# A hybrid decoder trunk on one core: every tile moved to another place in its memory row

## The chip, the cores and the metric

The kernel runs on one core of a Trainium2 chip. The metric is the time of one execution on the device, in microseconds (us). A core has five engines with instruction streams of their own: TensorE (PE in the profile; its weight loads have a row of their own, PEld), VectorE (DVE), ScalarE (ACT), GpSimd (POOL) and SyncE (SP). The on-chip memory has 128 partitions; a tile takes the same bytes in each of its partitions, so its place is one byte address, the same in all rows. PSUM is the memory that matmuls write.

A matmul has two operands in that on-chip memory: the *stationary* one, a block of up to 128x128 values that is loaded into the array by a weight load (LDWEIGHTS), and the *moving* one, up to 512 columns that stream past it (MATMUL). The profile names a matmul `out<-moving,stationary`: `acc<-whi,gh` streams a piece of the tile `whi` past a block of `gh`.

## The reference, cut to what matters

Two layers over 256 tokens of width 1024, in float32:

```
x = x + 0.5 * swiglu_ffn(x, ffn1)          # 1024 -> 2 x 2816 -> 1024
h = rms_norm(x);  z = h @ w_in             # one wide input projection
y = sum_i sigmoid(gate_i(h)) * (branch_i @ P_i)   # stick-breaking, latent, sparse attention
x = x + y @ w_out
x = x + 0.5 * swiglu_ffn(x, ffn2)
```

Nothing in the change touches what is computed.

## The kernel before, in words

**Products.** Each float32 product is made of three matmuls of a reduced type: every operand is held as a high part and a low remainder, and `mm3` (lines 528 to 532) issues high x high (L530), high x low (L531) and low x high (L532). In the large projections the activations are stationary and the weights move. So the stationary order within one `mm3` is: high block, high block again, low block; every one of the three has its own weight load.

**Stationary tiles.** The activations lie transposed, 128 values by 128 rows to a block, and each block is 512 bytes of a memory row: `hThi`, `hTlo` (`new_T`, L540; two buffers each) for the normed input of a block; `gh0`, `gl0`, `gh1`, `gl1` (L675) for the gated activation of an FFN; `oh`, `ol` (`new_oT`, L766) for the output of an attention branch; `cT` (L873) for the latent.

**Moving tiles.** Weights come as slabs of 128x1024 values. A slab arrives in `raw` tiles of 512 columns (L503, issued on SP's queue), ACT writes the high part into `whi` (L514, L817) and DVE the remainder into `wlo` (L515, L819); there are four buffers of each. In the mixer the probabilities `wr` move past `V`, and the scores' masks and constants lie in `rt`. A transpose is a matmul too: the data is stationary and `ident` moves.

**Order.** Each layer is FFN, mixer (attention), FFN. PE's instructions stand in the order in which the program writes them. In the mixer a planner works out one order for PE, ACT and DVE from its own cost estimates, and that order is fixed (a manual schedule); in the FFNs ACT's and DVE's order is left to the framework. None of the planner's costs looks at an address.

**Places.** Tiles are taken from pools, and pools lie behind one another in the memory row: `cp` (constants), `sm` (small statistics, five buffers of each of four kinds, 64 bytes each), `wp` (whi, wlo, raw), `hp` (rows of x, `hThi`, `hTlo`, `rn`), and then `fp` in an FFN or `mp` in a mixer, in the same space. Within a pool each kind of tile lies behind the last one. In `cp` there is one tile of 32 bytes, `g_col` (L408), the first layer's gain as a column, which ACT writes once (L413) and DVE reads for the first transposes (L555). All other sizes in front of `wp` add up so that with these 32 bytes every tile of `wp`, `hp`, `fp` and `mp` named above begins 32 bytes behind a multiple of 512.

The places, as the remainder of a tile's first byte by 512:

| tile | before | after |
|---|---|---|
| whi, wlo, raw, x, h, mq, nq, nk | 32 | 0 |
| ident | 320 | 320 |
| rt | 352 | 320 |
| hThi | 32 | 64 |
| hTlo | 32 | 128 |
| gh0, gl0 | 32, 32 | 192, 256 |
| gh1, gl1 | 32, 32 | 320, 384 |
| V, cT, zw | 32 | 128 |
| oh, ol | 32, 32 | 256, 320 |
| wf, wr, th, qk, pc, Vc | 32 | 320 |

The column "after" is the sum of the sizes that the diff leaves: 32 bytes less in front of everything, then the free spaces.

One group of matmuls has always had its stationary operand at another remainder than its moving one: the compressed scores of the sparse branch (L1668), whose stationary blocks are cut out of `zkh` and `zkl` at columns 32, 0, 128 and 96, while `nq` moves.

Of the kernel before, what the change touches and what calls it, by code (L numbers as in the profile page):

```python
# [10 lines left out]
F = mybir.dt.float32  # L11
R = mybir.dt.float32r
# [5 lines left out]
S = 256  # L18
DEPTH = 2
DFF = 2816  # L20
EPS = 1e-6
NT = 2
KT = D // 128
# [333 lines left out]
def decoder_trunk(ctx, tc, x_in, wts, gains, lcon, cst, out, depth=DEPTH):  # L357
# [4 lines left out]
    cp = ctx.enter_context(tc.tile_pool(name="cp", bufs=1))  # L362
    sm = ctx.enter_context(tc.tile_pool(name="sm", bufs=5))
    wp = ctx.enter_context(tc.tile_pool(name="wp", bufs=W_BUFS))
    hp = ctx.enter_context(tc.tile_pool(name="hp", bufs=2))
# [4 lines left out]
    def acc_tile():  # L370
        return pb.tile([128, 512], F, tag="ps", name="acc")

    def tp_tile():
        return pb.tile([128, 512], F, tag="ps", name="tp")

    def att_tile():
        return pb.tile([128, 512], F, tag="ps", name="att")

    def big_tile(name, dt=F, shape=(128, D)):
        return hp.tile(list(shape), dt, tag="hy", name=name, bufs=6)  # L380

# [18 lines left out]
    def load_x(t, cols=(0, 1)):  # L400
        for c in cols:
            cs = slice(c * 512, (c + 1) * 512)
            nc.sync.dma_start(xs[t][:, cs], x_in[t * 128:(t + 1) * 128, cs])


    g_row = big_tile("grow")[0:8, 0:128]
    nc.sync.dma_start(g_row, gains[0].rearrange("(k p) -> k p", k=8))
    g_col = cp.tile([128, 8], F, name="g_col")  # L408

    def first_gain():  # L410
        tp = tp_tile()
        nc.tensor.transpose(tp[:, 0:8], g_row, ident[0:8, 0:8])
        nc.scalar.activation(g_col, tp[:, 0:8], AF.Copy)  # L413
# [93 lines left out]
    def load_slab():  # L507
        base, n, name = slab_at(pos[0])
        pos[0] += 1
        hi, lo = slab_tiles()  # L510
        for c in range(0, n, RAW):
            m = min(RAW, n - c)
            raw = load_raw(base, c, m)
            nc.scalar.activation(hi[:, c:c + m], raw[:, :m], AF.Copy)  # L514
            nc.vector.tensor_tensor(lo[:, c:c + m], raw[:, :m], hi[:, c:c + m], op=OP.subtract)  # L515
        return name, (hi, lo)

    def next_slab():
        while pos[0] < len(stream) and len(ready) < 1 + AHEAD:
            ready.append(load_slab())  # L520
        return ready.pop(0)[1]


    def split(hi, lo, src):
        nc.scalar.activation(hi, src, AF.Copy)  # L525
        nc.vector.tensor_sub(lo, src, hi)  # L526

    def mm3(o, a, b, start=False, stop=False):

        nc.tensor.matmul(o, a[0], b[0], start=start, stop=False)  # L530
        nc.tensor.matmul(o, a[0], b[1], start=False, stop=False)  # L531
        nc.tensor.matmul(o, a[1], b[0], start=False, stop=stop)  # L532
# [5 lines left out]
        return r  # L538

    def new_T():  # L540
        return (hp.tile([128, KT, 128], R, tag="hThi", name="hThi"),
                hp.tile([128, KT, 128], R, tag="hTlo", name="hTlo"))

    def to_T(dst, src, halves=(0, 1), tmp=None):

        for half in halves:
            tp = tp_tile()
            for j in range(4):
                k = half * 4 + j
                nc.tensor.transpose(tp[:, j * 128:(j + 1) * 128], src[:, k * 128:(k + 1) * 128], ident)  # L550
            k = slice(half * 4, half * 4 + 4)
            v = tp.rearrange("p (a b) -> p a b", a=4)
            if tmp is not None:
                u = tmp[:, half * 512:half * 512 + 512].rearrange("p (a b) -> p a b", a=4)
                nc.vector.tensor_tensor(u, v, g_col[:, k, None].to_broadcast([128, 4, 128]), op=OP.mult)  # L555
                v = u
            split(dst[0][:, k, :], dst[1][:, k, :], v)
# [19 lines left out]
    def enter():  # L577

        return [big_tile("h") for _ in range(NT)], [new_T() for _ in range(NT)], [None] * NT
# [71 lines left out]
    def ffn(l, gi):  # L651
        if l == 0 and gi == 0:
            nxt[0] = hs, hT, rn = enter()
            gain_n[0] = 1
            first_gain()
            ready.append(load_slab())
            load_x(0, (1,))
            to_T(hT[0], xs[0], tmp=hs[0])
            sl = [next_slab()]
            load_x(1)  # L660
            for t in range(NT):
                rn[t] = norm_scale(t)
            h1 = dict(tmp=hs[1])
            hs = [None, xs[1]]
            steps = [(0, 0, 0), (0, 0, 1), (0, 1, 0), (1, 0, 0), (1, 0, 1), (1, 1, 0), (0, 1, 1), (1, 1, 1)]
            h1_at = (2, 0), (2, 2)
        else:
            sl = []
            steps = [(t, part, q) for t in range(NT) for part in range(2) for q in range(2)]
            h1_at = (2, 0), (2, 3)  # L670
            hs, hT, rn = nxt[0]
            h1 = {}
        with ExitStack() as es:
            fp = es.enter_context(tc.tile_pool(name="fp", bufs=2))
            gT = [(fp.tile([128, DFF // 128, 128], R, name=f"gh{t}", bufs=1),  # L675
                   fp.tile([128, DFF // 128, 128], R, name=f"gl{t}", bufs=1)) for t in range(NT)]
            todo = []

            def glu(t, a, b, f0, fn):
                s = fp.tile([128, 512], F, tag="sil", name="sil")  # L680
                nc.scalar.activation(s[:, :fn], a[:, :fn], AF.Silu, scale=rn[t][:, 0:1])
                g = fp.tile([128, 512], F, tag="g", name="g", bufs=3)
                nc.vector.scalar_tensor_tensor(g[:, :fn], b[:, :fn], rn[t][:, 0:1], s[:, :fn], op0=OP.mult, op1=OP.mult)  # L683
                todo.append((t, g, f0, fn))

            def flush():
                if todo:
                    t, g, f0, fn = todo.pop(0)
                    tp = tp_tile()
                    q = fn // 128  # L690
                    for j in range(q):
                        nc.tensor.transpose(tp[:, j * 128:(j + 1) * 128], g[:, j * 128:(j + 1) * 128], ident)  # L692
                    k0 = f0 // 128
                    split(gT[t][0][:, k0:k0 + q, :], gT[t][1][:, k0:k0 + q, :],
                          tp[:, :fn].rearrange("p (a b) -> p a b", a=q))

            f0, fn = FFN_CHUNKS[0]
            g = KT // 2
            assert g * fn == 1024
            sl += [next_slab() for _ in range(4 - len(sl))]  # L700
            ab = {}
            for i, (t, part, q) in enumerate(steps):
                if q == 0:
                    ab[t, part] = acc_tile()
                a = ab[t, part]
                for k in range(q * g, q * g + g):
                    if (i, k) in h1_at:
                        to_T(hT[1], hs[1], (h1_at.index((i, k)),), **h1)
                    mm3(a[:, :fn], cut(hT[t], A, k, A),
                        cut(sl[part * 2 + q], A, slice((k % g) * fn, (k % g + 1) * fn)),  # L710
                        start=k == 0, stop=k == KT - 1)
                if part == 1 and q == 1:
                    glu(t, ab[t, 0], a, f0, fn)

            def hook(i):
                if i in (3, 5):
                    flush()

            for ci, (f0, fn) in enumerate(FFN_CHUNKS[1:]):
                if ci == 1:  # L720
                    with tc.issue_after(last_dma[0]):
                        if l == 0 and gi == 0:
                            load_consts()
                        load_gain()
                        if gi == 0:
                            load_lc(l)
                if ci == 3 and gi == 0:
                    make_tables()
                a = {}
                drain(chunk(fn, KT, hT, a.__setitem__), hook)  # L730
                drain(chunk(fn, KT, hT, lambda t, b: glu(t, a[t], b, f0, fn)))

            def between(k):
                if k in (2, 3):
                    flush()
            out_rows(gT, DFF // 128, between, last=l == depth - 1 and gi == 2)


    def mixer(l):
        es = ExitStack()  # L740
        mp = es.enter_context(tc.tile_pool(name="mp", bufs=1))
# [21 lines left out]
        def bc(a, H):  # L763
            return a[:, None, :].to_broadcast([a.shape[0], H, a.shape[-1]])

        def new_oT():  # L766
            return (mp.tile([128, 4, S], R, tag="oh", name="oh", bufs=2),
                    mp.tile([128, 4, S], R, tag="ol", name="ol", bufs=2))

        last_act = []  # L770

# [100 lines left out]

        cT = mp.tile([128, 2, NT, 3, 128], R, tag="r3", name="cT")  # L873
        cT = cT[:, 0], cT[:, 1]
        o_sb, o_mla, o_nsa = new_oT(), new_oT(), new_oT()
        small = mp.tile([128, 256], F, name="small")
        krg = [small[:, 56 * t:56 * t + 56] for t in range(NT)]
        ev_hT, ev_rn, ev_cT, ev_krg = events(2), [Tok(2.0), Tok(4.0)], events(NT), events(NT)
# [950 lines left out]
```

## Time and profile before

| what | value |
|---|---|
| three runs | 1319.73, 1321.48, 1323.20 us; median 1321.48 us |
| the profiled execution | 1320.05 us, of which the span of the core is 1318.3 us |
| PE busy | 1294.1 us, 98% of the span |
| DVE busy, ACT busy | 893.3 us (68%), 796.4 us (60%) |
| granted TensorE clock | 0.997 over the span |
| DMA | mean 175 GB/s; the main queue's packets take 53.7% of 16 engines' span |

A busy PE is not PE at its peak: matmuls are pipelined, and the duration of one in the profile (some 390 ns for 512 columns) is longer than the distance from its start to the next one's start. Where PE has no wait, that distance is what sets the time, so the timeline (start, duration, instruction) is read by differences of its first column.

### The profile page before, as it was taken

To read this page: it belongs to the slowest core of one execution; us is meant where nothing else is said; L and a number is where in the kernel's file an instruction comes from. 1 tells how busy PE (TensorE), PEld (TensorE's weight loads), DVE (VectorE), ACT (ScalarE), POOL (GpSimd) and SP (SyncE) were. 2 spreads that over 40 slices of the span, in tenths; PEclk is the share of its full clock that TensorE was granted. 3 is DMA by queue.
4 is the path that set the end of the run, shared out by engine and by line. 5 is a ranking of instruction groups with operands and counts; after the bars stand their busy time and mean duration, and the time that the engine had idled before them with its cause. 6 is when DMAs were issued, how large, how long until landed. Compare 5 with 4: busy or idle time off the path is not lost.

```text
span 1318.3 us, 19987 instructions
## 1 busy us (share of the span) xinstructions
PE 1294.1 (98%) x6623; PEld 1078.1 (82%) x6623; DVE 893.3 (68%) x1852; ACT 796.4 (60%) x1654; POOL 43.3 (3%) x50
## 2 busy tenths in 40 slices
PE   7999999999899999999999999999989999999998
PEld 6888888888777888888888888888878778888887
DVE  6655557988987775555566554679879876755553
ACT  5545447796888555454464544478868884645542
POOL 0000000210000000000000000011100000000000
PEclk9999999999999999999999999999999999999999
DMA  6755556535424556555556555565453355555653
GB/s 230 245 189 178 192 183 225 179 124 176 129 91 132 186 171 204 190 178 191 192 180 215 182 190 185 192 215 161 135 174 110 102 160 176 175 185 184 190 185 120
DMA packets 124504, 230.77 MB, mean 175 GB/s; under 512 B 13928, under 2 KB 15600, under 8 KB 124400
## 3 DMA queue, kind: packets, MB, share of 16 engines
q1 hardware_dynamic: 124144, 228.97, 53.7%
q8 instruction: 52, 0.85, 0.2%
q0 software_dynamic: 256, 0.52, 0.1%
q14 instruction: 52, 0.43, 0.1%
HBM read 225.77 MB, written 3.15 MB: 174 GB/s over the span
## 4 chain that ended last, share of the span: by engine, by line
PE 84%; ACT 7%; DVE 6%; issue 2%; DMA 0%; SPq 0%; DVEq 0%; ACTq 0%
PE acc L530 26%; PE acc L532 26%; PE acc L531 26%; ACT wf L1341 2%; ACT whi L817 2%; PE tp L692 1%; DVE wlo L819 1%; ACT wf L1368 1%; DVE wr L1385 1%; DVE wlo L515 1%; DVE x L626 1%; PE att L1291 1%; PE att L1727 1%; DVE wf L1351 1%; PE tp L1377 1%
## 5 line engine op out<-in xcount | busy, mean ns | idle before, releaser
L515 DVE TENSOR_TENSOR wlo<-raw,whi 128x512 fp32r<-128x512 f32 (+1 forms) x560 | 362.0, 688 | 311.5 <-ACT whi L514 310.0
L514 ACT ACTIVATE whi<-raw 128x512 fp32r<-128x512 f32 (+1 forms) x560 | 322.9, 623 | 368.5 <-PE acc L532 361.7
L530 PE MATMUL acc<-whi,hThi 128*128 128x512 f32 (+2 forms) x1248 | 480.2, 385 | 0.5 <-ACT hThi L525 0.5
L532 PE MATMUL acc<-whi,hTlo 128*128 128x512 f32 (+2 forms) x1248 | 470.1, 377 | 0.4 <-DVE hTlo L526 0.4
L531 PE MATMUL acc<-wlo,hThi 128*128 128x512 f32 (+2 forms) x1248 | 469.0, 376 | 0.0
L532 PEld LDWEIGHTS acc<-whi,hTlo 128*128 128x128 f32 x1248 | 235.4, 189 | 44.1 <-DVE hTlo L526 0.9
L530 PEld LDWEIGHTS acc<-whi,hThi 128*128 128x128 f32 x1248 | 235.8, 189 | 39.2 <-ACT hThi L525 1.0
L531 PEld LDWEIGHTS acc<-wlo,hThi 128*128 128x128 f32 x1248 | 236.1, 189 | 37.6
L819 DVE TENSOR_TENSOR wlo<-raw,whi 128x512 fp32r<-128x512 f32 (+1 forms) x276 | 181.4, 681 | 41.7 <-ACT whi L817 40.5
L817 ACT ACTIVATE whi<-raw 128x512 fp32r<-128x512 f32 (+1 forms) x276 | 162.9, 619 | 53.3 <-PE acc L532 42.7
L530 PE MATMUL acc<-whi,gh 128*128 128x512 f32 x352 | 138.3, 393 | 0.0
L532 PE MATMUL acc<-whi,gl 128*128 128x512 f32 x352 | 137.1, 390 | 0.0
L531 PE MATMUL acc<-wlo,gh 128*128 128x512 f32 x352 | 136.9, 389 | 0.0
L532 PEld LDWEIGHTS acc<-whi,gl 128*128 128x128 f32 x352 | 66.1, 188 | 13.9
L531 PEld LDWEIGHTS acc<-wlo,gh 128*128 128x128 f32 x352 | 66.1, 188 | 13.4
L530 PEld LDWEIGHTS acc<-whi,gh 128*128 128x128 f32 x352 | 66.1, 188 | 13.2
L537 POOL TENSOR_TENSOR rs<-ss,mh 128x1 f32<-128x1 f32 (+4 forms) x30 | 36.6, 1221 | 1027.8 <-DVE ss L536 1005.6
L1341 ACT ACTIVATE wf<-wf,mn 128x128 f32<-128x128 f32 x96 | 42.7, 446 | 12.0 <-DVE mn L1351 11.5
L530 PE MATMUL acc<-whi,oh 128*128 128x512 f32 x96 | 41.3, 430 | 0.5 <-DVE y L1157 0.5
L531 PE MATMUL acc<-wlo,oh 128*128 128x512 f32 x96 | 38.6, 402 | 0.0
L532 PE MATMUL acc<-whi,ol 128*128 128x512 f32 x96 | 38.5, 401 | 0.0
L683 DVE SCALAR_TENSOR_TENSOR g<-acc,rn,sil 128x512 f32<-128x512 f32 (+1 forms) x48 | 33.6, 702 | 2.9 <-PE acc L532 0.8
(274 smaller groups left out, 1262.5 us busy)
## 6 DMA issues: line engine op xcount, KB each, us to landing
raw<-in_wts SPq DMA_DIRECT2D x824, 256.0 KB, 2.7
gain<-in_gains SPq DMA_DIRECT2D x5, 512.0 KB, 5.6
xd<-x SPq DMA_DIRECT2D x4, 512.0 KB, 4.5
x<-xd SPq DMA_DIRECT2D x4, 512.0 KB, 4.2
raw<-in_wts SPq DMA_DIRECT2D x8, 184.0 KB, 2.6
lc<-in_lcon SPq DMA_DIRECT2D x2, 528.0 KB, 7.6
x<-in_x SPq DMA_DIRECT2D x4, 256.0 KB, 5.1
out_dram<-x SPq DMA_DIRECT2D x4, 256.0 KB, 2.0
```

The costliest lines, as they stand in the source:

```text
L514: nc.scalar.activation(hi[:, c:c + m], raw[:, :m], AF.Copy)
L515: nc.vector.tensor_tensor(lo[:, c:c + m], raw[:, :m], hi[:, c:c + m], op=OP.subtract)
L530: nc.tensor.matmul(o, a[0], b[0], start=start, stop=False)
L531: nc.tensor.matmul(o, a[0], b[1], start=False, stop=False)
L532: nc.tensor.matmul(o, a[1], b[0], start=False, stop=stop)
L537: nc.gpsimd.tensor_tensor(r[:p, :w], ss[:p, :w], mh[:p, :w], op=OP.pow)
L626: nc.vector.scalar_tensor_tensor(xv, accs[t, c], 0.5, xv, op0=OP.mult, op1=OP.add)
L683: nc.vector.scalar_tensor_tensor(g[:, :fn], b[:, :fn], rn[t][:, 0:1], s[:, :fn], op0=OP.mult, op1=OP.mult)
L692: nc.tensor.transpose(tp[:, j * 128:(j + 1) * 128], g[:, j * 128:(j + 1) * 128], ident)
L817: nc.scalar.activation(hl[0][:, c:c + m], raw[:, :m], AF.Copy)
L819: nc.vector.tensor_tensor(hl[1][:, c:c + m], raw[:, :m], hl[0][:, c:c + m], op=OP.subtract)
L1341: nc.scalar.activation(E[i][:, cs], E[i][:, cs], AF.Exp, scale=-1.0, bias=mn[:, q:q + 1], accum_out=su[:, q:q + 1])
```

## The change

`g_col` leaves the pool of constants and becomes part of a 64-byte tile of the kind `mn` in the pool `sm`, which already has five such buffers. A new helper, `space`, takes a tile that nothing writes or reads. It is called ahead of `hThi` (64 bytes) and `hTlo` (64), once in the whole program; ahead of each of the four gated tiles in an FFN (64 each); and in a mixer ahead of `oh` (128) and `ol` (64). No instruction of the computation is added, removed or moved in the text of the kernel.

```diff
+    def space(pool, name, n):
+
+        pool.tile([128, n // 4], F, tag=name, name=name, bufs=1)
...
-    g_col = cp.tile([128, 8], F, name="g_col")
+    g_col = sm.tile([128, 16], F, tag="mn", name="g_col")[:, 0:8]
...
     def new_T():
-        return (hp.tile([128, KT, 128], R, tag="hThi", name="hThi"),
-                hp.tile([128, KT, 128], R, tag="hTlo", name="hTlo"))
+        if not spaced:
+            space(hp, "gap0", 64)
+        hi = hp.tile([128, KT, 128], R, tag="hThi", name="hThi")
+        if not spaced:
+            space(hp, "gap1", 64)
+            spaced.append(True)
+        return hi, hp.tile([128, KT, 128], R, tag="hTlo", name="hTlo")
+
+    spaced = []
...
-            gT = [(fp.tile([128, DFF // 128, 128], R, name=f"gh{t}", bufs=1),
-                   fp.tile([128, DFF // 128, 128], R, name=f"gl{t}", bufs=1)) for t in range(NT)]
+            gT = []
+            for t in range(NT):
+                pair = []
+                for q in "hl":
+                    space(fp, f"gap{q}{t}", 64)
+                    pair.append(fp.tile([128, DFF // 128, 128], R, name=f"g{q}{t}", bufs=1))
+                gT.append(tuple(pair))
...
-        def new_oT():
-            return (mp.tile([128, 4, S], R, tag="oh", name="oh", bufs=2),
-                    mp.tile([128, 4, S], R, tag="ol", name="ol", bufs=2))
+        def new_oT(n=0):
+            if n:
+                space(mp, "gapo", 128)
+            hi = mp.tile([128, 4, S], R, tag="oh", name="oh", bufs=2)
+            if n:
+                space(mp, "gapl", 64)
+            return hi, mp.tile([128, 4, S], R, tag="ol", name="ol", bufs=2)
...
-        o_sb, o_mla, o_nsa = new_oT(), new_oT(), new_oT()
+        o_sb, o_mla, o_nsa = new_oT(1), new_oT(), new_oT()
```

## The prediction

> **What bounds the kernel now.** I read the page first: span, busy shares, and the chain of waits.
>
> ```profile
> span 1318.3 us, 19987 instructions
> PE 1294.1 (98%) x6623; PEld 1078.1 (82%) x6623; DVE 893.3 (68%) x1852; ACT 796.4 (60%) x1654; POOL 43.3 (3%) x50
> PEclk9999999999999999999999999999999999999999
> PE 84%; ACT 7%; DVE 6%; issue 2%; DMA 0%; SPq 0%; DVEq 0%; ACTq 0%
> ```
>
> PE is busy nearly all the time at a full granted clock, and 84% of the chain that ends last is PE itself; DMA has none of it. So the time is the number of matmuls times the distance between their starts, and a change of places alone can matter only if it changes that distance. The second view is the groups by line with shapes kept apart, for the counts.
>
> ```profile
> L530 PE MATMUL acc<-whi,hThi 128*128 128x512 f32 x1056 | 421.3, 399 | 0.0
> L530 PE MATMUL acc<-whi,gh 128*128 128x512 f32 x352 | 138.3, 393 | 0.0
> L530 PE MATMUL acc<-whi,hThi 128*128 128x256 f32 x160 | 46.9, 293 | 0.5 <-ACT hThi L525 0.5
> L530 PE MATMUL acc<-whi,oh 128*128 128x512 f32 x96 | 41.3, 430 | 0.5 <-DVE y L1157 0.5
> L1377 PE MATMUL tp<-ident,wf 128*128 128x128 f32 x144 | 25.4, 286 | 9.4 <-ACT wf L1368 9.0
> ```
>
> L531 and L532 have the same counts as L530, so there are 3 x (1056 + 352 + 96) = 4512 matmuls of 512 columns and 3 x 160 = 480 of 256 columns, each with a weight load of its own. The distances come from the timeline of PE. Its rows are start, duration, instruction. First a clean stretch of the last FFN (115 rows from the first to the last shown), then one of 48 rows with 256 columns:
>
> ```profile
> 1285.15 0.39 PE L530 MATMUL acc<-whi,gh 128*128 128x512 f32 x1
> ...
> 1310.99 0.39 PE L530 MATMUL acc<-whi,gh 128*128 128x512 f32 x1
> ```
>
> ```profile
> 300.07 0.28 PE L530 MATMUL acc<-whi,hThi 128*128 128x256 f32 x1
> 300.19 0.28 PE L531 MATMUL acc<-wlo,hThi 128*128 128x256 f32 x1
> ...
> 305.70 0.28 PE L532 MATMUL acc<-whi,hTlo 128*128 128x256 f32 x1
> ```
>
> (1310.99 - 1285.15) / 114 = 226.7 ns for 512 columns, (305.70 - 300.07) / 47 = 119.8 ns for 256. The 256 further columns cost 106.9 ns, 0.4176 ns each; what is left is 226.7 - 213.8 = 12.9 ns per matmul that does not grow with its columns. In both stretches the moving and the stationary tile begin 32 bytes behind a multiple of 512: they have distance 0. **The question of this case is whether those 12.9 ns depend on the two places.**
>
> **What the trace shows of other places.** Three groups already have another distance. (a) In the latent projection a slab holds two blocks of 440 columns, so every second block begins 1760 bytes further on, at remainder 256: an aligned place, at distance 288 from the stationary one. The rows are the first matmul of each block of three.
>
> ```profile
> 205.18 0.36 PE L530 MATMUL acc<-whi,hThi 128*128 128x440 f32 x1
> ...
> 205.78 0.36 PE L530 MATMUL acc<-whi,hThi 128*128 128x440 f32 x1
> ...
> 206.38 0.36 PE L530 MATMUL acc<-whi,hThi 128*128 128x440 f32 x1
> ...
> 209.98 0.39 PE L530 MATMUL acc<-whi,hThi 128*128 128x512 f32 x1
> ```
>
> The block at remainder 32 takes 0.60 us, the one at 256 takes 0.60 us, and the whole (24 matmuls in 4.80 us) 200.0 ns each. Neither the aligned start nor the distance changes anything.
>
> (b) In the stick-breaking scores the stationary `rt` has distance 320 from what moves:
>
> ```profile
> 269.98 0.39 PE L532 MATMUL acc<-whi,hTlo 128*128 128x512 f32 x1
> 270.20 0.22 PE L1290 MATMUL att<-wr,rt 128*128 128x128 f32 x1
> 270.26 0.39 PE L1291 MATMUL att<-wr,rt 128*128 128x384 f32 x1
> 270.49 0.22 PE L1290 MATMUL att<-wr,rt 128*128 128x128 f32 x1
> ```
>
> While the first row's 512 columns stream, `rt` is loaded at distance 320; the next start comes after 0.22 us, where every ordinary one comes after 0.227. A reduction worth speaking of is not there. The pair of 128 and 384 columns takes 0.29 us; twice 12.9 ns and 512 columns would be 0.24, so this place is no faster there, and perhaps slower.
>
> (c) In the compressed scores the distances are 64, 192, 320 and 448, all odd multiples of 64; twelve rows from the first to the last:
>
> ```profile
> 1023.09 0.28 PE L530 MATMUL acc<-nq,zkh 128*128 128x256 f32 x1
> 1023.20 0.28 PE L531 MATMUL acc<-nq,zkh 128*128 128x256 f32 x1
> ...
> 1024.34 0.28 PE L532 MATMUL acc<-nq,zkl 128*128 128x256 f32 x1
> ```
>
> (1024.34 - 1023.09) / 11 = 113.6 ns, 6.2 ns less than the 119.8 of the same shape at distance 0. This is the only row that speaks for the change. At 256 columns the weight load of 128 columns and the stream are about equally long, so a load that is disturbed can hold up the next start; at 512 it has twice the time.
>
> **The change part by part.** *The column of the gain* moves to a tile of another pool. Its write and its reads stay:
>
> ```profile
> 3.47 0.18 ACT L413 ACTIVATE g_col<-tp 128x8 f32<-128x8 f32 x1 [1.45 <-PE tp L412]
> 5.54 0.69 DVE L555 TENSOR_TENSOR h<-tp,g_col 128x512 f32<-128x512 f32 x1 [4.66 <-PE tp L550]
> ```
>
> No instruction more or less, and no wait: the buffer is wanted again only by the fifth `mn` tile, in the first mixer, some 200 us after the last read. 0 us. *The free spaces* are tiles that nobody writes: no instruction, no DMA, 0 us.
>
> *All places 32 bytes lower.* The transfers now begin on multiples of 512. Landing and the one place where a transfer sets the chain:
>
> ```profile
> raw<-in_wts SPq DMA_DIRECT2D x824, 256.0 KB, 2.7
> 3.50 4.91 DMA raw<-in_wts
> ```
>
> The 2.7 us are hidden: the chain gives DMA 0%. Only the first 4.91 us stand on the path; were a row of 2048 bytes that straddles one more 256-byte boundary a ninth slower, the gain is 4.91 / 9 = 0.5 us. I take 0, with 0 to 0.5 as bounds. The moving operands' start costs nothing by (a).
>
> *New distances for 512 columns.* They become 64 and 128 for `hThi` and `hTlo`, 192 to 384 for the gated tiles, 256 and 320 for `oh` and `ol`. By (a) and (b) 0 ns per matmul; the lower bound is (c)'s saving on each, 4512 x 6.2 ns = 28.0 us. The upper bound is a loss of the same step, 28.0 us, since no row excludes that distance 0 is the good place. I take 0: (b) is the row with 512 columns.
>
> *New distances for 256 columns.* `hThi` is two of the three loads and gets distance 64, which (c) has; `hTlo` gets 128, which no row has. 2/3 x 480 x 6.2 ns = 2.0 us of gain; bounds 0 and 3.0 us.
>
> *Other pairs.* `wf` against `ident`, and `wr` against `rt`, come to distance 0; `V` against `wr` leaves it. The 144 transposes of L1377 would lose at most 144 x 6.2 = 0.9 us. I take 0 for these together, within 0.9 us either way.
>
> *Waits.* None is added: the engines' orders are fixed or worked out from costs without addresses, and the tiles share buffers as before.
>
> Sum: the profiled execution's 1320.05 us (span 1318.3 and 1.75 outside) less 2.0 gives 1318.05. The median of the runs lies 1.43 above the profiled execution, so **1319.5 us**.
>
> The Trainium skill ("TensorE: Matmul & The Clock Gate", section "Step-by-step: what each phase is for") says that PE has two independent read ports and that loading the next weights does not take read bandwidth from the running matmul. By it no distance matters at all, and the sum would be 1321.5; (c) against the 256-column rows disagrees by 6.2 ns, (b) agrees. The same page ("Back-to-back issue gap") gives an isolated matmul of 512 columns some 215.8 ns, where the row has 226.7; if the whole difference of 10.9 ns came from places, an estimate by it would be 4512 x 10.9 = 49 us of gain.
>
> **The rivals.**
>
> *A: the load disturbs every stream.* The 12.9 ns are the same at 256 and 512 columns, as if each load took a fixed time from the stream beside it; then (c) shows that half of it goes when the places differ by an odd multiple of 64. Such distances get two of three `hT` loads, two of three gated ones (192, 320) and `ol`: 2 x 1056 + 2 x 352 + 96 = 2912 of 512 columns and 320 of 256, 3232 x 6.2 = 20.0 us: 1301.5; with all of them, 28.0 + 3.0 = 31 us: 1290.5. For it: (c), and the constant 12.9. Against it: (b) at 512 columns and (a), both at other distances and both without gain.
>
> *B: distance 0 is the good place.* A load and a stream that begin together keep out of each other's way; at other distances they meet later, and each matmul of 512 columns pays one more step of 6.2 ns: 28.0 us, 1349.5. It decides from 4.0 / 4512 = 0.9 ns per matmul on; with 2 ns it is 9.0 us less the 2.0 gained, 1328.5. For it: the pair in (b), 0.29 us against 0.24. Against it: that pair's 128 columns are shorter than a load, which explains a delay, and (a).
>
> *C: nothing moves.* (c) is quick for another reason than its places (its operands come from other pools), or the spaces do not shift what they should: 1321.5.
>
> **How the numbers follow.** I take 0.3%, 4.0 us, as what a measurement can tell from no change. Forecast (0 to 3 us of gain) 0.52; C 0.12; both are within 0.3%: 0.64. A in whole or in part 0.24, of which some 0.07 is a small part (1311 to 1317). B 0.12, most of it small. The likeliest's own range is 1317.5 to 1323. The range that leaves two in ten out takes A's small part and most of B: 1311 to 1329; outside lie the rest of A (0.17) and B's far end (0.03). Faster 0.24, same 0.64, slower 0.12.
>
> **What would show it.** In the clean stretch of the last FFN the starts stay 226.7 ns apart (forecast, C); 220.5 would be A, over 227.6 B. The 256-column run goes from 119.8 to some 115.7 (two loads of three at 113.6), or stays (C). The latent projection stays at 200. L1377's transposes and the waits of PE stay as they are. A new wait on `mn`, or a changed order on ACT or DVE in an FFN, would make the working wrong in its part on waits.

## The result, and the profile after

The changed kernel takes 1336.23 us (median of five runs, 1333.95 to 1337.58) where the kernel before takes 1321.48 us (five runs, 1319.73 to 1323.20): a ratio of 1.0114, with a 95% interval of 1.0102 to 1.0125. That is 14.75 us more, outside the range of the prediction and on the side that it had given a chance of 0.12.

The page of the kernel after, the same lines as were read of before:

```profile
span 1335.8 us, 19987 instructions
PE 1311.6 (98%) x6623; PEld 1080.7 (81%) x6623; DVE 894.3 (67%) x1852; ACT 796.2 (60%) x1654; POOL 42.3 (3%) x50
PEclk9999999999899999999999999999999999999999
PE 84%; ACT 7%; DVE 6%; issue 2%; DMA 0%; SPq 0%; ACTq 0%; DVEq 0%
```

The instruction counts are the same, the granted clock is the same but for one slice, and no engine's share of the chain has moved. PE is busy 17.5 us longer (1311.6 - 1294.1), and the span is 17.5 us longer. DVE and ACT are busy as before, within 1 us. So no new wait has come: the same matmuls take longer. (The two profiled executions lie 17.5 us apart, where the medians lie 14.75 apart: that of before took 1320.05 us, 1.4 below its median, and that of after, 1337.58 us, is the longest of its five.) The groups with shapes kept apart (columns: busy us, the sum of the durations; mean ns of one; then the idle time before them) say which:

```profile
L534 PE MATMUL acc<-whi,hThi 128*128 128x512 f32 x1056 | 428.5, 406 | 0.0
L536 PE MATMUL acc<-whi,hTlo 128*128 128x512 f32 x1056 | 414.6, 393 | 0.0
L535 PE MATMUL acc<-wlo,hThi 128*128 128x512 f32 x1056 | 412.5, 391 | 0.0
L534 PE MATMUL acc<-whi,gh 128*128 128x512 f32 x352 | 140.2, 398 | 0.0
L536 PE MATMUL acc<-whi,gl 128*128 128x512 f32 x352 | 138.7, 394 | 0.0
L535 PE MATMUL acc<-wlo,gh 128*128 128x512 f32 x352 | 137.7, 391 | 0.0
L534 PE MATMUL acc<-whi,hThi 128*128 128x256 f32 x160 | 47.6, 297 | 0.3 <-ACT hThi L529 0.3
L534 PE MATMUL acc<-whi,oh 128*128 128x512 f32 x96 | 41.4, 432 | 0.4 <-DVE y L1177 0.4
L1397 PE MATMUL tp<-ident,wf 128*128 128x128 f32 x144 | 25.4, 286 | 9.0 <-ACT wf L1388 8.8
```

The lines of the code stand four further down; L534 to L536 are `mm3`. In before the rest of these groups read:

```profile
L532 PE MATMUL acc<-whi,hTlo 128*128 128x512 f32 x1056 | 412.5, 391 | 0.0
L531 PE MATMUL acc<-wlo,hThi 128*128 128x512 f32 x1056 | 411.5, 390 | 0.0
L532 PE MATMUL acc<-whi,gl 128*128 128x512 f32 x352 | 137.1, 390 | 0.0
L531 PE MATMUL acc<-wlo,gh 128*128 128x512 f32 x352 | 136.9, 389 | 0.0
```

By difference, the 3168 matmuls with `hThi` and `hTlo` cost 7.2 + 2.1 + 1.0 = 10.3 us more, the 1056 gated ones 1.9 + 1.6 + 0.8 = 4.3 us more, those with `oh` and `ol` 1.1 us (119.5 for 118.4 in their three groups), and those of 256 columns 1.6 us (140.4 for 138.8): 17.3 us in all. The last two don't belong to the distances for certain: in profiles of the experiments below that have `oh` and `ol` at distance 0 or 256 their groups take 118.1 to 120.2 us, and the 256 columns take 138.1 us in a kernel with the very distances of after and 141.2 us in one with all distances at 256. The transposes of L1397 and their waits stand where they stood (25.4 us, 286 ns).

The timeline of PE (start, duration, instruction) shows the same thing where nothing interrupts it: 118 rows of the last FFN from the first to the last shown, and 48 rows with 256 columns.

```profile
1297.27 0.39 PE L534 MATMUL acc<-whi,gh 128*128 128x512 f32 x1
...
1324.31 0.40 PE L534 MATMUL acc<-whi,gh 128*128 128x512 f32 x1
```

```profile
306.36 0.28 PE L534 MATMUL acc<-whi,hThi 128*128 128x256 f32 x1
...
311.93 0.28 PE L536 MATMUL acc<-whi,hTlo 128*128 128x256 f32 x1
```

(1324.31 - 1297.27) / 117 = 231.1 ns between starts, where it was 226.7; (311.93 - 306.36) / 47 = 118.5 ns, where it was 119.8. The prediction had named "over 227.6" as the sign of its rival B, that distance 0 is the good place.

### The profile page after: what moved, and what is told of

It reads as the page before. It is cut to its first block, busy times and chain, and to the rows that moved or that the text cites. A ratio compares the mean times of both kernels' runs of the same rounds, so it can differ in the third digit from the quotient of the medians.

```text
span 1335.8 us, 19987 instructions
## 1 busy us (share of the span) xinstructions
PE 1311.6 (98%) x6623; PEld 1080.7 (81%) x6623; DVE 894.3 (67%) x1852; ACT 796.2 (60%) x1654; POOL 42.3 (3%) x50
## 4 chain that ended last, share of the span: by engine, by line
PE 84%; ACT 7%; DVE 6%; issue 2%; DMA 0%; SPq 0%; ACTq 0%; DVEq 0%
PE acc L534 26%; PE acc L536 26%; PE acc L535 26%; ACT wf L1361 2%; ACT whi L837 2%; PE tp L708 1%; ACT wf L1388 1%; DVE wlo L839 1%; DVE wr L1405 1%; DVE wlo L519 1%; DVE x L637 1%; PE att L1311 1%; PE att L1747 1%; PE tp L1397 1%; DVE wf L1371 0%
## 5 line engine op out<-in xcount | busy, mean ns | idle before, releaser
L534 PE MATMUL acc<-whi,hThi 128*128 128x512 f32 (+2 forms) x1248 | 487.9, 391 | 0.3 <-ACT hThi L529 0.3
L536 PE MATMUL acc<-whi,hTlo 128*128 128x512 f32 (+2 forms) x1248 | 472.5, 379 | 0.6 <-DVE hTlo L530 0.4
L536 PEld LDWEIGHTS acc<-whi,hTlo 128*128 128x128 f32 x1248 | 236.0, 189 | 51.4 <-DVE hTlo L530 1.1
L534 PEld LDWEIGHTS acc<-whi,hThi 128*128 128x128 f32 x1248 | 236.0, 189 | 40.0 <-ACT hThi L529 0.6
L534 PE MATMUL acc<-whi,gh 128*128 128x512 f32 x352 | 140.2, 398 | 0.0
L536 PE MATMUL acc<-whi,gl 128*128 128x512 f32 x352 | 138.7, 394 | 0.0
L536 PEld LDWEIGHTS acc<-whi,gl 128*128 128x128 f32 x352 | 66.2, 188 | 15.5
L534 PEld LDWEIGHTS acc<-whi,gh 128*128 128x128 f32 x352 | 66.0, 188 | 14.1
L534 PE MATMUL acc<-whi,oh 128*128 128x512 f32 x96 | 41.4, 432 | 0.4 <-DVE y L1177 0.4
L536 PE MATMUL acc<-whi,ol 128*128 128x512 f32 x96 | 39.2, 409 | 0.0
```

## The experiments

Two readings of the result stood against each other at first. **Theory D**: the distance between the first byte of the stationary block and that of the moving rows decides, and 0 is good. **Theory P**: the place itself decides. A third, **N**, was that it takes the kernel around it: traffic of other engines that meets PE at the new places.

### Matmuls alone, at every distance

Nothing runs here but matmuls. Each group is 18 to 24 of them on one pair of operands, with no wait; the rest of the decoder is left out.

```diff
+    def run(name, items):
+        o = pb.tile([128, 512], F, tag="ps", name=name)
+        for i, (n, m, a, s) in enumerate(items):
+            nc.tensor.matmul(o[:, 0:n], st[:, s // 4:s // 4 + 128], mo[m][:, a // 4:a // 4 + n],
+                             start=i == 0, stop=i == len(items) - 1)
...
+    for i in range(32):
+        run("a" + code(i), [(512, 0, 0, 16 * i)] * 18)
+    for i, sh in enumerate((4, 8, 16, 32, 64, 128, 256)):
+        run("b" + code(i), [(512, 0, sh, sh)] * 18)
...
```

> This kernel leaves the whole decoder out; its output is the input x. It streams weights past stationary blocks with nothing else running, in groups of 18 to 24 matmuls, each group with one distance between the stationary block's place and the moving block's (512 columns: 0 to 496 bytes in steps of 16; 256 columns: 0 to 480 in steps of 32), with distance 0 at other absolute places, and with the kernel's own threes of distances. Theory D (the distance decides): 226.7 ns per start at distance 0 whatever the absolute place, some 228 to 236 ns at 64 to 384, no change where 512 bytes are added; the threes (64, 64, 128) about 231 ns on average. Theory P (the absolute place decides): all groups of 512 columns alike in the first set, and a difference among the groups with distance 0. Theory N (neighbours on ACT, DVE and DMA are needed for the loss): every group of 512 columns at 226.7.

The groups of this kernel, by name: `aaa` is distance 0, `aab` 16 bytes, `aae` 64, `aam` 192, `aap` 240, `aaq` 256; `bag` has both operands 256 bytes further on, with distance 0.

```profile
L42 PE MATMUL aaa<-mhi,st 128*128 128x512 f32 x18 | 4.2, 389 | 0.0
L42 PE MATMUL aab<-mhi,st 128*128 128x512 f32 x18 | 4.2, 389 | 0.0
L42 PE MATMUL aae<-mhi,st 128*128 128x512 f32 x18 | 4.4, 395 | 0.0
L42 PE MATMUL aam<-mhi,st 128*128 128x512 f32 x18 | 4.3, 392 | 0.0
L42 PE MATMUL aap<-mhi,st 128*128 128x512 f32 x18 | 4.2, 389 | 0.0
L42 PE MATMUL aaq<-mhi,st 128*128 128x512 f32 x18 | 4.2, 389 | 0.0
L42 PE MATMUL bag<-mhi,st 128*128 128x512 f32 x18 | 4.2, 389 | 0.0
```

What the profile gives as a duration lies some 162 ns (160 to 163) above the distance between two starts, in each group of 512 columns here, so its differences can be read as differences of the starts, within some 2 ns. The starts themselves, worked out from the trace as a mean of each group without its first three:

```
512 columns, distance in bytes: ns from start to start
  0, 16, 240, 256, 272, 496 : 226.6
  192, 448                  : 228.9
  176, 432                  : 230.4
  80, 336                   : 231.8
  all the other multiples of 16: 233.1 to 234.3
the kernel's threes, distance of high / low block:
  0/0  226.7   64/128  231.2   192/256  230.3   320/384  231.2   256/320  230.9   256/256  226.7
```

Three things follow. The loss is there with nothing else running, so N isn't needed. The pattern repeats after 256 bytes, and what is good is a distance of 0 or 256, or 16 to either side of it. And the four pairs of distances that the change gives to its stationary tiles cost 3.6 to 4.5 ns a matmul: the 230.3 and 231.2 of the two gated pairs are on average 230.8, and the last FFN after has 231.1.

The prediction cited the Trainium skill ("TensorE: Matmul & The Clock Gate", section "Step-by-step: what each phase is for") for two independent read ports, by which no distance matters. Here the measurement decides: 226.6 against 233.3 ns, with a load and a stream as the only traffic.

### The parts of the change, one by one

Four kernels take the change apart. The first moves `g_col` alone; the second leaves it and has the spaces alone; the third has only the gated tiles displaced, to 192, 256, 320 and 384; the fourth only `hThi` and `hTlo`, to 64 and 128, with the gated tiles, `V`, `cT`, `oh` and `ol` behind them brought back to distance 0. What lies behind `small` in the mixer (`wf`, `wr`, `th`, `qk`, `pc`, `Vc`) begins at 128 in that kernel, not at 0; the groups in which `wr` moves past `V` take 58.2 us there and 58.0 us in before.

```diff
 # 1
-    g_col = cp.tile([128, 8], F, name="g_col")
+    g_col = sm.tile([128, 16], F, tag="mn", name="g_col")[:, 0:8]
 # 2: all of the change but this line
 # 3: on the kernel before
+                    space(fp, f"gap{q}{t}", 64 if q != "h" or t else 192)
 # 4: on 1
+            space(hp, "gap0", 64)          # ahead of hThi
...
+            space(hp, "gap1", 64)          # ahead of hTlo
...
+            space(fp, "gap2", 384)         # FFN: behind them, back to 0
...
+        space(mp, "gap2", 384)             # mixer: the same
...
-        small = mp.tile([128, 256], F, name="small")
+        small = mp.tile([128, 160], F, name="small")
```

> The first half of the change alone: the gain column moves, so that every tile begins on a multiple of 512 and all distances stay 0. Theory D: as before, ratio 1.000 within 0.002. Theory P: as the changed kernel, ratio 1.011. If transfers that begin on a multiple of 512 mattered, up to 0.5 us faster.

> The second half alone: the free spaces, with the gain column where it was, so that the moving tiles begin 32 bytes behind a multiple of 512 as before and the distances are those of the changed kernel (64 and 128, 192 to 384, 256 and 320). Theory D: ratio 1.011, starts of 235, 228 and 229 ns in the large projections as in the changed kernel. Theory P: ratio 1.000.

> Only the four gated tiles of the FFNs get other distances (192, 256, 320, 384), everything else stays as before. Theory D: the loss of L530 to L532 with gh and gl alone, which is 4.2 us by the sums of the starts in the two traces: ratio 1.0032. Theory P: ratio 1.000, since no moving tile is displaced. If other tiles (oh, V, wf against ident) made the loss, 1.000 as well.

> Only hThi and hTlo are displaced (to 64 and 128); everything behind them is brought back to distance 0. Theory D, with the 233 to 235 ns of the starts that a hThi at 64 leaves and the 228 of hTlo at 128: 8.7 + 2.4 us for 512 columns and 1 us for 256, so +11 to +12 us, ratio 1.0083 to 1.0092. The rival, that the loss belongs to the whole arrangement and not to each displaced tile: the gated tiles alone gave 4.2 us and all spaces 14.0, so anything under 7 us (ratio below 1.0053) or over 14 us would speak for it.

| displaced | median us | ratio to before, 95% interval | more than before, us |
|---|---|---|---|
| nothing (`g_col` moved: all places on multiples of 512) | 1320.51 | 0.9996 (0.9988 to 1.0005) | -0.6 |
| all, without the alignment | 1335.51 | 1.0111 (1.0096 to 1.0127) | +14.4 |
| the gated tiles | 1325.69 | 1.0034 (1.0021 to 1.0046) | +4.6 |
| `hThi` and `hTlo` | 1330.88 | 1.0075 (1.0063 to 1.0088) | +9.3 |

Each is set against the runs of the kernel before that it shared a chip with. The alignment is worth nothing that can be told; the spaces alone give the whole loss; and the two parts of it add up: 4.6 + 9.3 = 13.9 us, with 0.5 left for the tiles of the mixer. Their groups carry it one by one. The gated tiles alone (L534 to L536 of that kernel):

```profile
L534 PE MATMUL acc<-whi,hThi 128*128 128x512 f32 x1056 | 421.4, 399 | 0.0
L534 PE MATMUL acc<-whi,gh 128*128 128x512 f32 x352 | 140.2, 398 | 0.0
L536 PE MATMUL acc<-whi,gl 128*128 128x512 f32 x352 | 138.7, 394 | 0.0
```

`hThi` and `hTlo` alone:

```profile
L534 PE MATMUL acc<-whi,hThi 128*128 128x512 f32 x1056 | 428.4, 406 | 0.0
L536 PE MATMUL acc<-whi,hTlo 128*128 128x512 f32 x1056 | 414.5, 393 | 0.0
L534 PE MATMUL acc<-whi,gh 128*128 128x512 f32 x352 | 138.4, 393 | 0.0
```

The displaced group has the time that it has in the full change (398 and 394; 406 and 393), the other the time it had before (399; 393). The last of the four missed its expectation a little: +11 to +12 us had been named and +9.3 was measured, in part since the 256 columns, entered there with 1 us of loss, took 138.2 us in all three groups instead of 138.8: a small gain.

### One distance for all

These three put one space ahead of all stationary tiles and none between them, so that high and low blocks have a common distance of 256, 448 or 64. They tell D from the theory that only *unlike* distances side by side cost, and they test the period.

```diff
+    space(hp, "gap", 256)      # or 448, or 64
-    g_col = cp.tile([128, 8], F, name="g_col")
+    g_col = sm.tile([128, 16], F, tag="mn", name="g_col")[:, 0:8]
```

> One space of 256 bytes ahead of every stationary tile and none between them: every stationary tile has distance 256 from the moving weights. Theory D with a period of 256 bytes: nothing is lost, ratio 1.000 (0.999 to 1.001), and the starts in the last FFN stay 226.7 ns apart. The rival, that distance 0 itself is needed (a period of 512): 4512 x 4 to 6.6 ns = 18 to 30 us, ratio 1.014 to 1.023.

> The same with a space of 448 bytes: one distance of 448 (64 bytes short of the next 512) for every stationary tile. Theory D with the earlier measured 228.9 ns at 192 and 448: 4512 x 2.25 ns = 10.2 us, ratio 1.0077 (1.006 to 1.009). The rival, that only unlike distances side by side (64 and 128, 192 and 256) cost and a common one does not: ratio 1.000.

> One space of 64 bytes ahead of every stationary tile and none between: one distance of 64 for all. The matmuls alone gave 233.3 ns at 64 beside 226.65 at 0, so theory D says 4512 x 6.65 = 30.0 us, ratio 1.0227, and starts of 233 ns in the last FFN. If the kernel turns only a part of that into time, as with 448 (4.4 us for 10.2), 13 us, ratio 1.010. The rival, that only unlike distances side by side cost: ratio 1.000.

| distance of all | median us | ratio, 95% interval | more than before, us |
|---|---|---|---|
| 256 | 1321.14 | 0.9999 (0.9990 to 1.0008) | -0.4 |
| 448 | 1325.93 | 1.0037 (1.0024 to 1.0049) | +4.4 |
| 64 | 1345.17 | 1.0168 (1.0148 to 1.0188) | +23.1 |

The timeline of PE in the last FFN, first with all at 256 (140 rows), then with all at 64 (136 rows):

```profile
1284.64 0.39 PE L535 MATMUL acc<-whi,gh 128*128 128x512 f32 x1
...
1316.15 0.39 PE L536 MATMUL acc<-wlo,gh 128*128 128x512 f32 x1
```

```profile
1307.72 0.40 PE L536 MATMUL acc<-wlo,gh 128*128 128x512 f32 x1
...
1339.22 0.39 PE L536 MATMUL acc<-wlo,gh 128*128 128x512 f32 x1
```

31.51 / 139 = 226.7 ns and 31.50 / 135 = 233.3 ns: in a clean stretch the kernel does what the matmuls alone did, to the tenth. So the place doesn't count (all tiles at 256 are as good as at 0), the distance does, and a common distance of 64 is worse than the change's own spread. P falls, and so does the theory of unlike distances.

The sizes of the two losses were missed: 448 gave 4.4 us for an expected 10.2, and 64 gave 23.1 for 30.0. The kernel isn't a clean stretch throughout. Its groups with all at 64:

```profile
L535 PE MATMUL acc<-whi,hThi 128*128 128x512 f32 x1056 | 426.4, 404 | 0.0
L537 PE MATMUL acc<-whi,hTlo 128*128 128x512 f32 x1056 | 417.3, 395 | 0.0
L536 PE MATMUL acc<-wlo,hThi 128*128 128x512 f32 x1056 | 417.1, 395 | 0.0
```

In before the three groups took 399, 391 and 390 ns, where the matmuls alone take 389: some of their starts were late already. PE issues the same matmuls in the same order in all these kernels, so the traces can be set beside each other start by start. Of the 4512 matmuls of 512 columns, 4328 have another one of them right behind. In before, 3260 of these took 226 to 228 ns to the next start. The same 3260 take 6.6 ns more each with all at 64 (21.6 us), 2.2 ns more with all at 448 (7.3 us) and 4.4 ns more in after (14.4 us): the price that the matmuls alone had. The 820-odd that took 228 to 250 ns in before, 232 on average, lose next to nothing by it: all together they take 0.7 us more with all at 64 (233 ns each, like the others there), 1.7 us less at 448 and 0.4 us less in after. So the price per start was right, and the count of 4512 was not: a start that already takes as long as the bad distance would make it has nothing to lose. What made those starts late in before, no run separates. A gain with 256 columns, which is in these traces too, is spoken of below.

### What a single displaced load does, and other widths

> Matmuls alone again; the decoder is left out, the output is x. Theory D in two forms. D-load: the loss belongs to each displaced load and grows with its width. Loads of 32, 64, 96 columns (aaa to aaf, distance 0 and 64 in turn, 512 columns) then give at 64 some 228.3, 230.0, 231.6 ns beside 226.6 at 0; one displaced load in 12, 6, 3, 2 (baa to bad) gives means of 227.2, 227.7, 228.9, 230.0 ns. D-pattern: the loss comes only where displaced loads follow one another; baa to bad all give 226.6, and the prediction's row (b), one displaced load among many at 0, was blind for that reason. 256 columns as in the kernel (caa to cad: high/low distances 0/0, 64/64, 448/320, 64/128) and with the twelve distances of the compressed scores (cae): if places explain row (c), cae gives 113.6 and caa 119.8 ns; if not, cae gives 117 to 118. 440 columns, moving start 0 or 1760, several distances (daa to daf): 200 ns for all, as no loss showed at that width. Distance 0 for 72 matmuls at starts 32, 64, 128 (eaa to eac): 226.7 once settled by D; 227.5 to 229 if the start itself counts. Distances 4 to 28 and 228 to 244 (faa to faj): 226.6 up to 16, over 231 from 20 or 24 and at 228 to 236; starts off a multiple of 16 bytes may cost by themselves. Widths 452 to 504 (gaa to gal, distance 0 and 64): no loss at 480, 6.6 ns at 512; D does not say whether it comes in a step or steadily.

```diff
+    for i, every in enumerate((12, 6, 3, 2)):
+        run("b" + code(i), [(512, 0, 0, 64 if k % every == every - 1 else 0) for k in range(36)])
...
+    for i, n in enumerate((452, 464, 472, 488, 496, 504)):
+        run("g" + code(2 * i), [(n, 0, 0, 0)] * 24)
+        run("g" + code(2 * i + 1), [(n, 0, 0, 64)] * 24)
```

The decoder is left out again. One load at distance 64 among eleven at 0 gives this row of starts, worked out from the trace, over and over, each value from one start to the next; the first ends with the start of the displaced matmul itself:

```
226, 236, 228, 233, 231, 226, 227, 227, 226, 227, 227, 226
```

The displaced matmul starts on time. The one behind it comes 9 ns late, and only after four starts is the pace back at 226.7. One such load costs 20 ns altogether (twelve starts take 2740 ns for 2720), three times the 6.7 ns that each costs where all are displaced. One in six costs 20 ns each as well (mean 230.0), one in three 13 ns (231.0), one in two 6.7 ns (230.0). So neither form of the theory held: single loads cost, against D-pattern, and they cost more than where all are displaced, against D-load.

The price isn't in proportion to the load's width either. Loads of 32 columns give 231.7 ns at distance 0 and at 64 alike, loads of 64 columns 230.3 and 232.7, loads of 96 columns 230.0 at 0 and 228.4 at 64. And 0 is the good distance for 512 columns, not for every width:

```
columns         440    464    488    496    504    512
distance 0    200.0  210.0  220.0  223.4  226.7  226.7
distance 64   200.1  213.4  220.1  220.0  228.9  233.3
```

At 440 columns nothing shows (nor at 452, 472 and 480), at 496 distance 64 is 3.4 ns *better*. Many of the steady rates lie about 3.3 ns apart (220.0, 223.4, 226.7, 230.0, 233.3), but not all: 228.9 and 231.7 lie between. With distance 0 at starts of 32, 64 and 128 bytes the pace comes to 226.7 within eleven starts and stays: the 227.4, 228.2 and 228.9 of the first measurement were the way there. Distances that aren't a multiple of 16 cost even between good ones, against the expectation: 4, 8 and 12 give 232.4, 230.7 and 230.0, and 20 and 244 give 233.3. With 256 columns the twelve distances of the compressed scores gave 113.4 ns and distance 0 gave 119.6, as if places did explain row (c) of the prediction; that is what the next experiment takes apart.

### 256 columns

> Matmuls of 256 columns alone; the decoder is left out, the output is x. The last measurement gave 113.4 ns with the twelve distances of the compressed scores and 117.8 to 120.0 with every constant distance. What makes it? Theory Q (a change between distances 64 and 192): groups baa to bad, which change between them every 1, 2, 3 or 6 matmuls at one fixed moving tile, give 113.4 in at least one case, and bae to bah (0 with 128 or 64) do not. Theory M (the places of the blocks themselves): only aaa, aab and gaa to gae, which use the blocks of the compressed scores, give 113.4. Theory R (moving tiles that advance): aaa gives 113.4 and aab, with one fixed moving tile, 117 or more. Groups caa to cam and daa to dae displace the moving weights of 256 columns and keep the stationary blocks at 0, which a kernel could do without touching its 512 columns: if one of them gives 113.4, a version with 480 x 6.4 = 3.1 us of gain (ratio 0.998) follows; if none does, there is at most 480 x 2 = 1 us to be had.

```diff
+    for i, q in enumerate(((64, 192), (64, 64, 192, 192), (64, 64, 64, 192, 192, 192), (64,) * 6 + (192,) * 6,
+                           (0, 128), (0, 64), (0, 0, 0, 64, 64, 64), (0, 0, 0, 128, 128, 128), (64, 320))):
+        run("b" + code(i), [(256, 0, 0, q[k % len(q)]) for k in range(36)])
...
+    for i, s0 in enumerate((0, 256, 512, 1024, 2048, 2304)):
+        run("e" + code(i), [(256, 0, 0, 64 + (s0 if k % 2 else 0)) for k in range(36)])
```

The decoder is left out here too. A change between 64 and 192 does give 113.3 ns, but so does a constant distance of 64 (`eaa`), which had given 117.8 in the first measurement. `bai` and `eab` settle it: both change between 64 and 320 on the same bytes, in the same order, 36 times. Their rows in the timeline (start, time of the whole run):

```profile
52.59 4.41 PE L44 MATMUL bai<-mhi,st 128*128 128x256 f32 x36
```

```profile
111.85 4.24 PE L44 MATMUL eab<-mhi,st 128*128 128x256 f32 x36
```

(4.41 - 0.28) / 35 = 118.0 ns, (4.24 - 0.28) / 35 = 113.1 ns. What differs is what ran before them, and the PSUM bank that they write; but `eaf`, which writes the bank of `bai` and changes between the same two distances (on other bytes), runs at 113.3, so the bank isn't it. At these distances 256 columns have two steady rates, 117.8 and 113.3, and each of the two groups keeps its own for all its 36 matmuls. That what ran before decides is what is left; which part of it does, no run shows. So the numbers that theory Q had named did come, and its reason falls all the same, since no change between distances is needed; M falls with `baa` to `bad`, and R with `aab`, which gave 113.4 with a fixed moving tile.

The decoder's own compressed scores say the same. They run once in each layer, on the same places in both. The prediction quoted the second layer's; here is the first layer's in before (twelve rows), and both in after:

```profile
371.02 0.28 PE L530 MATMUL acc<-nq,zkh 128*128 128x256 f32 x1
...
372.30 0.28 PE L532 MATMUL acc<-nq,zkl 128*128 128x256 f32 x1
```

```profile
378.38 0.28 PE L534 MATMUL acc<-nq,zkh 128*128 128x256 f32 x1
...
379.63 0.28 PE L536 MATMUL acc<-nq,zkl 128*128 128x256 f32 x1
...
1037.35 0.28 PE L534 MATMUL acc<-nq,zkh 128*128 128x256 f32 x1
...
1038.65 0.28 PE L536 MATMUL acc<-nq,zkl 128*128 128x256 f32 x1
```

Before: 116 ns in the first layer, 113.6 in the second. After: 113.6 and 118.2. The distances of this group didn't change, and its pace did, in both directions. The 116 ns is a mean of both rates: worked out from the trace, the eleven starts are 118, 118, 114, 117, 123, 118, 113, 114, 113, 113 and 114 ns apart. So a group can also pass from the one to the other.

No version that beats the kernel before was run. With 512 columns nothing went below the 226.6 that it has. With 256 columns displaced weights against stationary blocks at 0 gave 116.0 at best, 480 x (119.8 - 116.0) = 1.8 us, not much more than the 1.1 us to which eleven runs of this kernel tell a difference. The quick rate can be had in the decoder: in the kernel with all at 64 the starts of 256 columns have medians of 113 to 114 ns in the four FFNs and 118 in the two mixers, where before has 120 in all of them, some 2 us against the 23 that its 512 columns lose. Whether weights displaced for the 256 columns alone would give that rate in the decoder stays open.

## Why the prediction was wrong, step by step

**What bounds the kernel** was right: PE alone, its matmuls' starts. The loss is busy time of PE in groups whose counts didn't change, 14.6 us of it in those of `hThi`, `hTlo` and the gated tiles, and nothing on DMA, DVE or ACT.

**The step that failed** is "New distances for 512 columns", in its words "By (a) and (b) 0 ns per matmul", and "I take 0: (b) is the row with 512 columns". The runs show 3.6 to 4.5 ns for each in clean stretches, and 14.4 us over the 3260 starts that ran at 226 to 228 ns before. The reason given with (c), that the load has twice the time at 512 columns and so can't hold up the next start, falls with it: alone, 512 columns lose 6.7 ns at distance 64, and 256 columns lose nothing (117.8 or 113.3 ns, where distance 0 has 120.0). Both rows that the step rested on were read rightly and said nothing on the question:

- (a), the latent projection, has 440 columns. At that width matmuls alone show no difference either (200.0 and 200.1 ns at 0 and 64), while at 512 the same distance costs 6.7. A row of one width was carried to another as though the loss had to be there at both or neither.
- (b) read the start of the displaced matmul itself, 0.22 us after the one before it. A displaced load leaves its own start on time and delays the next ones (226, then 236). And the displaced matmuls of (b) come in pairs of 128 and 384 columns, widths that lose little: alone, 128 columns take 111.5 ns at distance 0 and 111.8 at 64 (192 columns take the same, so it isn't the columns that set it), and 384 take 174.1 and 176.7. Together that is 0.29 us at either distance, the time of the pair; the 0.24 us that it was held against left this out. So the pair was neither evidence for rival B nor against it; it could not show the loss.

**New distances for 256 columns**, 2.0 us of gain from (c): a third of it at most came. In the stretch where 115.7 ns was forecast the starts are 118.5 ns apart, 1.3 ns less than before, which is 0.6 us over 480; alone, distances of 64 and 128 gave 118.3 too. The 1.6 us that the three groups take longer in the profile lie in the first 16 us of the span, where starts of some 213 ns stand in these traces: 31 of the starts of 256 columns took 200 ns or more there, against 21 in before, and 31 also with all tiles at 256, where the distances cost nothing. (c) was one of two occurrences of the same instructions on the same places, and the other, 116 ns in the first layer, was in the trace of before to be read. It measured one of two rates in which the group can run, and not a place alone. The bounds worked out from it, 28.0 us up and down, held the truth all the same, by luck: 6.2 ns isn't far from the 6.7 that distance 64 costs.

**Rival B** was the way it went, and its clause "it decides from 0.9 ns per matmul on" was met. Its full price of 28.0 us was too high, since the change's distances cost 3.6 to 4.5 ns and the starts that were late already lose next to nothing; its small form (2 ns, 1328.5) was too low. Its mechanism, that a load and a stream that begin together keep out of each other's way, fits 512 columns at 0 and 256, and doesn't fit 496 columns, where 64 is better.

**Rival A** falls: no distance takes anything off the 12.9 ns at 512 columns. So does **C** in both its forms: the spaces shift what they should, and distances matter. The constant 12.9 ns at both widths, from which A drew its strength, isn't a constant: 256 columns run at 113.3, 117.8 or 120.0.

**The steps costed at nothing** hold: the column of the gain and the alignment together are worth -0.6 us (interval -1.6 to +0.7), the spaces as such cost nothing (all at 256: -0.4 us), the transposes of L1397 stay at 286 ns, the latent projection at 200 ns, and no wait is added. The latent's own tile `cT`, which the list of new distances leaves out, went to 128, and its groups take 25.8 us for 25.5. The 0.5 us thought possible in the first transfer didn't come: the chain's first piece in after is

```profile
3.50 5.32 DMA raw<-in_wts
```

where it was 4.91.

## What to carry to other kernels

When a stream of matmuls has a weight load for each, the places of the two operands are a tuning knob, here of up to 1.7%: with 512 columns of four bytes keep stationary and moving tiles a multiple of 256 bytes apart, wherever they lie. A row of the trace bears on a change only if it has the same width and the same steady repetition as the changed work; a single case, another width, or one of two occurrences can be true and blind. A cost below the page's resolution in a stream of 4500 is best measured alone, in a kernel of nothing but that stream: here one such run gave the loss of each distance. Such a price holds for the starts that run at full pace; count those, and not all.

## What the runs showed of the hardware

- The pace of matmuls with a load each depends on the distance of the two operands in the memory row, with a period of 256 bytes: 226.6 ns at 0, 228.9 at 192 and 233.3 at 64, for 512 columns.
- A displaced load is felt one start later, for four starts, and costs 20 ns where one in six or twelve is displaced, but 6.7 ns where all are (512 columns, distance 64).
- The same bytes in the same order can run at two steady rates (113.3 and 117.8 ns with 256 columns), as far as the runs tell by what ran before. Which part of the core keeps this state, and why many rates lie 3.3 ns apart, no run here shows.
- The good distance is one of the width: at 440 columns no distance tried changed the 200 ns, at 496 distance 64 ran at 220.0 ns and distance 0 at 223.4.
- Starts that took 228 to 250 ns at distance 0 already (232 on average) took 233 at distance 64: the price of 6.6 ns was paid by those at 226.7 alone.
- Operands that both begin 4, 8 or 16 bytes behind a multiple of 512, at distance 0, ran at 237.6, 231.1 and 231.1 ns over the eighteen matmuls of a group. Whether they come to 226.7 later, as starts of 32 to 128 bytes do, wasn't measured.
